# A second tiny write, from the first y tile into rows of the last output tile, in an interleaving copy kernel

## Chip, cores and metric

One core of one Trainium2 chip. The metric is the device time of one execution in microseconds (us). The core ran alone.

## The reference

```
x, y: (32, 256, 1024) float32
result[..., 0::2] = x
result[..., 1::2] = y          # (32, 256, 2048) float32
```

There is no arithmetic: 33.55 MB are read from x, 33.55 MB from y, and 67.11 MB are written. The values only have to change places, which VectorE does in SBUF.

## The kernel before

The flat arrays are cut into 8 tiles of 128 partitions x 8192 elements. Each tile is loaded with one DMA for x and one for y (4 MB each, on SP's queue, called q1 in the profile), interleaved in two halves by VectorE with two strided copies each, and stored with one DMA for each half (4 MB each, on ACT's queue, q10). Every pool has two buffers.

```
xpool, ypool, opool: bufs=2
zero = wpool.tile([16, 128]); nc.vector.memset(zero, 0.0)
first = out rows 0..15 of the first tile, 128 elements (512 B) each
nc.scalar.dma_start(out=first, in_=zero)          # the early tiny write

for lw in lwidths:                                 # 8 tiles
    xtile, ytile = ...
    nc.sync.dma_start(out=xtile, in_=xs)
    nc.sync.dma_start(out=ytile, in_=ys)
    for each half (soff = 0, 4096):
        otile = opool.tile([P, 2 * WS])
        nc.vector.tensor_copy(out=otile[:, 0::2], in_=xsub)
        nc.vector.tensor_copy(out=otile[:, 1::2], in_=ysub)
        nc.scalar.dma_start(out=os_, in_=otile)
# ... (the first x load is moved ahead of the opening barrier)
```

The framework adds the semaphores: a load waits until the buffer's last reader is done (the third y load goes out at 26.52 us, the copies that read its buffer end at 26.50), and a store to rows that an earlier DMA wrote waits until that one has landed.

Of the kernel before, what the change touches and what calls it, by code (L numbers as in the profile page):

```python
# [2 lines left out]

# [4 lines left out]


@with_exitstack
def _interleave(
    ctx: ExitStack,
    tc: tile.TileContext,
    x: bass.AP,
    y: bass.AP,
    out: bass.AP,
):
    nc = tc.nc
    P = 128  # L20

    total = 1
    for s in x.shape:
        total *= s

    WL = 8192
    WS = 4096

    xf = x.rearrange("b s d -> (b s d)")
    yf = y.rearrange("b s d -> (b s d)")  # L30
    of = out.rearrange("b s d -> (b s d)")

    fp32 = mybir.dt.float32

    xpool = ctx.enter_context(tc.tile_pool(name="xp", bufs=2))
    ypool = ctx.enter_context(tc.tile_pool(name="yp", bufs=2))
    opool = ctx.enter_context(tc.tile_pool(name="op", bufs=2))

    lwidths = [WL] * (total // P // WL)
    assert sum(lwidths) == total // P  # L40


    wpool = ctx.enter_context(tc.tile_pool(name="wp", bufs=1))
    zero = wpool.tile([16, 128], fp32, name="zero")
    nc.vector.memset(zero, 0.0)  # L45
    first = dataclasses.replace(of, offset=0, ap=[[2 * WL, 16], [1, 128]])
    nc.scalar.dma_start(out=first, in_=zero)

    start = 0
    for lw in lwidths:  # L50
        xtile = xpool.tile([P, WL], fp32, name="xtile")[:, :lw]
        ytile = ypool.tile([P, WL], fp32, name="ytile")[:, :lw]

        xs = dataclasses.replace(xf, offset=start, ap=[[lw, P], [1, lw]])
        ys = dataclasses.replace(yf, offset=start, ap=[[lw, P], [1, lw]])
        nc.sync.dma_start(out=xtile, in_=xs)
        nc.sync.dma_start(out=ytile, in_=ys)

        soff = 0
        while soff < lw:  # L60
            width = min(WS, lw - soff)
            otile = opool.tile([P, 2 * WS], fp32, name="otile")[:, : 2 * width]
            os_ = dataclasses.replace(
                of,
                offset=2 * start + 2 * soff,
                ap=[[2 * lw, P], [1, 2 * width]],
            )
            xsub = xtile[:, soff : soff + width]
            ysub = ytile[:, soff : soff + width]
# [3 lines that stand above are left out]
            soff += width  # L73

        start += P * lw
    assert start == total


def kernel(tc, x, y, out):
    nc = tc.nc  # L80
    _interleave(tc, x, y, out)
    tc.close()
    tc.compile()  # L83


    blocks = nc.main_func.blocks
    opening = blocks[0].instructions
    at, moved = next(
        (b, i)
        for b in blocks[1:]  # L90
        for i in b.instructions
        if i.engine == mybir.EngineType.SP and i.opcode == "DMACopy"
    )
    assert not moved.sync_info.on_wait
    body = at.instructions
    body.remove(moved)
    gate = next(
        n
        for n, i in enumerate(opening)
        if i.engine == mybir.EngineType.SP and i.opcode == "Drain"  # L100
    )
    opening.insert(gate, moved)
    at.instructions = body
    blocks[0].instructions = opening


# [1 line left out]
_INS = ['x', 'y']  # L108
_OUTS = [((32, 256, 2048), 'float32')]


# [23 lines left out]
```

## Time and profile before

| | before |
|---|---|
| time, median of the first 3 runs | 315.98 us (315.83 to 316.15) |
| span of the profiled execution | 313.8 us |
| busy VectorE | 23% |
| time of the packets on q1 + q10, share of 16 DMA engines | 49.9% + 49.5% |
| third y load issued | 26.52 us |
| first store issued | 24.32 us |

In profile lines DVE is VectorE, POOL GpSimd, SP SyncE and ACT ScalarE; a q behind the name (SPq) means the engine's instruction sequencer, which issues its DMAs, and L56 is line 56 of the kernel. A packet is one row of a DMA, here 32 KB for a full one (the trace before has 4096 of these, 128 for each of the 32 large DMAs), carried by one of the 16 DMA engines; a DMA lands when all its packets are done (the last packet of the first y load, one of 4 bytes, starts at 21.62 us, and the load lands at 21.97).

### The profile page before, as it was taken

What the parts mean: (1) busy time and instruction counts of PE and PEld (TensorE: products, weight loads), DVE (VectorE), ACT (ScalarE), POOL (GpSimd) and SP (SyncE); (2) the same over time, 40 slices, a digit from 0 to 9 for tenths busy, and PEclk for the clock granted to TensorE, in tenths of its full rate; (3) what the DMA queues carried; (4) which work ended last, traced back from release to release, by engine and by line L of the source; (5) the groups of instructions that cost most, each with busy time, mean ns of one, the idle gap of its engine ahead of it and who ended that gap; (6) DMA issues with size and microseconds to landing.
All of it is one profiled execution on the core that took longest, in us unless ns stands there. A gap on an engine that the chain in (4) does not pass through costs nothing.

```text
span 313.8 us, 152 instructions
## 1 busy us (share of the span) xinstructions
DVE 72.8 (23%) x33; POOL 0.2 (0%) x4
## 2 busy tenths in 40 slices
DVE  0433002231032410325003150130501305023500
POOL 0000000000000000000000000000000000000000
DMA  8999999999999999999999999999999999999997
GB/s 339 464 405 397 468 401 464 405 464 405 464 405 464 405 459 409 451 418 451 418 434 434 430 439 426 443 413 455 401 468 401 468 401 468 401 468 401 464 405 334
DMA packets 4640, 134.23 MB, mean 428 GB/s; under 512 B 528, under 2 KB 544, under 8 KB 544
## 3 DMA queue, kind: packets, MB, share of 16 engines
q1 hardware_dynamic: 2304, 67.11, 49.9%
q10 hardware_dynamic: 2336, 67.12, 49.5%
HBM read 67.11 MB, written 67.12 MB: 428 GB/s over the span
## 4 chain that ended last, share of the span: by engine, by line
DMA 83%; DVE 11%; DVEq 1%; issue 0%
DMA out_dram<-otile 76%; DMA ytile<-in_y_dram 7%; DVE otile L71 6%; DVE otile L70 5%; DVEq L83 1%; DVEq L70 0%
## 5 line engine op out<-in xcount | busy, mean ns | idle before, releaser
L70 DVE COPY otile<-xtile 128x4096 f32<-128x4096 f32 x16 | 36.6, 2295 | 184.9 <-DMA out_dram<-otile 173.7
L71 DVE COPY otile<-ytile 128x4096 f32<-128x4096 f32 x16 | 36.6, 2292 | 39.8 <-DMA ytile<-in_y_dram 39.8
L45 DVE MEMSET zero<- 16x128 f32 x1 | 0.2, 165 | 0.9 <-PEq L119 0.9
L119 POOL MEMSET const-bfloat16-1.0<- 128x1 bf16 x1 | 0.1, 102 | 0.0
L119 POOL MEMSET const-uint8-127<- 128x1 uint8 x1 | 0.1, 102 | 0.0
L119 POOL MEMSET const-float32-0.0<- 128x1 f32 x1 | 0.1, 99 | 0.2 <-issue 0.2
L119 POOL MEMSET const-float32-1.0<- 128x1 f32 x1 | 0.1, 99 | 0.0
## 6 DMA issues: line engine op xcount, KB each, us to landing
out_dram<-otile ACTq DMA_DIRECT2D x16, 4096.0 KB, 29.1
xtile<-in_x_dram SPq DMA_DIRECT2D x8, 4096.0 KB, 43.6
ytile<-in_y_dram SPq DMA_DIRECT2D x8, 4096.0 KB, 60.7
out_dram<-zero ACTq DMA_DIRECT2D x1, 8.0 KB, 6.3
```

Of the source, the lines that this page charges most:

```text
L45: nc.vector.memset(zero, 0.0)
L70: nc.vector.tensor_copy(out=otile[:, 0::2], in_=xsub)
L71: nc.vector.tensor_copy(out=otile[:, 1::2], in_=ysub)
L83: tc.compile()
L119: nc = _bacc.Bacc("TRN2", target_bir_lowering=False, num_devices=1)
```

## The change

A second write of 16 rows of 512 B is issued on ACT's queue as soon as the first y tile lands. Its rows lie in the last output tile, whose real store overwrites them some 260 us later. The early write stays. No comment in the code gives a reason. The likely intent is to touch a far part of the output early, so that the real store finds it ready.

```
         nc.sync.dma_start(out=ytile, in_=ys)
+
+        if start == 0:
+            late = dataclasses.replace(
+                of, offset=2 * (total - P * WL), ap=[[2 * WL, 16], [1, 128]]
+            )
+            nc.scalar.dma_start(out=late, in_=ytile[:16, :128])
```

## The prediction

> **What bounds the kernel now.** I read the page first (busy rows, queues, chain), then the issues of the DMAs, then the waits, then the first 30 us as a timeline, then stretches of the span, and last the single packet records behind them.
>
> The two DMA queues come first, because no compute engine is busy for more than a quarter of the time:
>
> ```profile
> span 313.8 us, 152 instructions
> ...
> DVE 72.8 (23%) x33; POOL 0.2 (0%) x4
> ...
> DMA  8999999999999999999999999999999999999997
> ...
> q1 hardware_dynamic: 2304, 67.11, 49.9%
> q10 hardware_dynamic: 2336, 67.12, 49.5%
> ```
>
> The loads (q1) and the stores (q10) together take 49.9 + 49.5 = 99.4% of the time of all 16 DMA engines. The row of digits says the same: only the first and the last slice of 7.8 us are below nine tenths. What is left to win without moving fewer bytes or moving them faster is 0.6% of 313.8 us, about 1.9 us. The packet records confirm it: every full-size packet is one 32 KB row, it takes 1.213 us at its fastest and almost always, and each engine has 4096 / 16 = 256 of them, so 256 x 1.213 = 310.5 us. The first packet starts 1.0 us into the span and the last one ends 1.1 us before its end; the remaining 1.2 us are 16 slow first packets and one hitch of which more below.
>
> The rate does not depend on the mix of loads and stores, which the stretches show (columns: stretch, length, busy VectorE, busy GpSimd, clock, DMA share, GB/s):
>
> ```profile
> 30.00:70.00 40.00, 7.10 (x4) 0.00 (x0) 1.00 1.00 433
> ...
> 148.00:224.00 76.00, 16.72 (x8) 0.00 (x0) 1.00 1.00 431
> 224.00:266.00 42.00, 11.97 (x6) 0.00 (x0) 1.00 1.00 431
> 266.00:298.00 32.00, 8.79 (x4) 0.00 (x0) 1.00 1.02 440
> ```
>
> In steady state loads and stores alternate; in the last of these stretches the loads run out (the last y tile lands at 287.67) and the rate stays. So shifting a load against a store by a few microseconds changes the order of the work and not its sum, as long as neither queue's lack of work empties an engine. The timeline agrees: the x load of a tile is issued at 69.81, 108.53, 147.26, 185.97 and 224.71, a period of 38.7 us for the 16.78 MB of a tile, 433 GB/s.
>
> The waits look different at first sight:
>
> ```profile
> DVE otile L70 <- DMA out_dram<-otile: 173.7, 14, 21.6
> DVE otile L71 <- DMA ytile<-in_y_dram: 39.8, 8, 5.2
> ```
>
> VectorE waits for stores and loads for most of the span. It is not the bottleneck, so these waits cost nothing by themselves: they are the DMA engines' backlog seen from the other side.
>
> [...]16 x 32768 B / 1.213 us = 432 GB/s while busy. [...]the tiny early write, issued on ACT's queue while loads run on SP's, has its 512 B packets at 5.3 to 5.9 us and its completion packets one load packet (1.2 us) later. [...]the tiny write took 6.3 us from issue to landing, because it stood behind 32 KB packets. The measured 6.3 is what I use. [...]the 16 packets of the early write took 27 ns each.
>
> **The change, part by part.** Nothing is removed. Added is one DMA on ACT's queue, from partitions 0 to 15 of the first y tile, 16 rows of 512 B (8 KB), into the first columns of 16 rows of the last output tile. The real store of that tile overwrites it much later.
>
> ```profile
> out_dram<-zero ACTq DMA_DIRECT2D x1, 8.0 KB, 6.3
> ...
> 1.06 0.42 ACTq L47 DMA_DIRECT2D out_dram<-zero  x1
> ...
> 16.80 0.33 SPq L56 DMA_DIRECT2D xtile<-in_x_dram  x1
> 22.00 4.50 DVE L71 COPY otile<-ytile 128x4096 f32<-128x4096 f32 x2 [5.22 <-DMA ytile<-in_y_dram]
> 24.32 2.56 ACTq L72 DMA_DIRECT2D out_dram<-otile  x2
> 26.52 0.33 SPq L57 DMA_DIRECT2D ytile<-in_y_dram  x1
> ```
>
> 1. Issue. The y tile lands at 21.97, when VectorE's copy (22.00) is released too. ACT's sequencer has nothing to do until the first store at 24.32, which waits for that copy. The new issue takes some 0.34 to 0.42 us (the other issues of ACT), so it is out at about 22.4, 1.9 us before the first store wants the sequencer. On the path: 0.
>
> 2. Work of the DMA engines. 16 rows over 16 engines is one packet each, 27 ns, and one completion packet, 9 ns (both as the early write's packets measure). That is 36 ns on each engine, and the engines are the bound, so it counts fully: +0.04 us.
>
> 3. A reader more on the first y buffer. The third y load, into the same buffer, is issued at 26.52 as soon as VectorE has read the tile. It must now also wait until the new write has read it, which is known only when that has landed. With the early write's 6.3 us that is 22.0 + 6.3 = 28.3, so this load is issued some 1.8 us later, at about 28.4. At that time SP's queue still holds the second x and y tiles and the third x tile, issued at 1.16, 1.63 and 16.80: 12.6 MB less what has gone (from 20 to 28 us about 3.4 MB), over 20 us of work for all engines. The late load lands behind them as before, about 94 us. SP's next issue is at 69.81. On the path: 0.
>
> 4. A second writer of the last tile's rows. The store of the first half of the last tile, at about 290 us, must wait for the new write, which has landed some 260 us before. 0.
>
> 5. Completion semaphores. DMAs take turns over eight semaphores, and each waits until the one eight places before has landed. The kernel issues four DMAs for each tile, so eight places back is the same kind of DMA two tiles back, with or without one DMA inserted near the start: only the first round changes partners, and these have landed long before. 0.
>
> Sum: 315.98 + 0.04 = 316.02 us, which I round to 316.0.
>
> **The rivals.**
> (a) The new wait on the y buffer becomes a real stall: the third y load is late and an engine runs dry. For it: it is a new wait of about 1.8 us and loads are issued in order. Against it: the backlog of over 20 us in step 3. If it bit, the time would be 317 to 318, still inside 2%.
> (b) The write takes away the hitch at the start of the stores, or causes another. In the packet records, the 16 load packets that start at 27.3 to 27.7 us take 1.69 to 1.88 us in place of 1.21; right after them, at 29.1, the first store packets begin. That is the only such place after the start, worth about 0.6 us on each engine. If an earlier write on the queue took that start upon itself, the time would be 315.4; if it made a second one, 316.6. Against both: the early tiny write was on the same queue at 5.3 us, and its neighbours took 1.21 us, so a tiny write neither causes the hitch nor spares it.
> (c) The intent of the change, I suppose, is that a page or row of the output touched early makes the first real store there cheaper. Against it: if first touches cost anything, the store packets of the tiles that nobody touched before would show it, and from 29.1 us to the end no full-size packet, load or store, took over 1.4 us. There is nothing to warm. Gain 0.
> (d) The first store waits for the new write, too, because the dependence between the two is taken too coarsely: it would go out at about 28.4 in place of 24.3. Against it: stores to other rows do not wait for each other now. Even so, loads would fill the engines meanwhile, the stores would be 4 us behind in order, and the end would move by little: 316.0 to 317.
>
> **Range and chances.** The three runs before spread from 315.83 to 316.15, so a median is good to 0.15 us or so. Around 316.0 I leave 0.6 us for the hitch of (b) on either side and lean slightly upwards for (a) and (d): 315.5 to 316.6. Faster by 2% would need 6.3 us, over three times what the idle share of the engines holds; I give it 0.003. Slower by 2% needs 6.3 us of idle engines, or a slower rate for all packets, from one DMA of 8 KB; I give it 0.007. Within 2%: 0.99.
>
> **What would show it.** In the profile of the changed kernel: a DMA of 8 KB on ACT's queue issued at 22.0 to 22.1 and landing 5 to 7 us later; the first store still issued at 24.3; the third y load at 28 to 29 us with a wait on the new write; q10 with 2368 packets (32 more: 16 of data, 16 of completion) and the shares of q1 and q10 still 99.4% together; x loads from the fourth on still 38.7 us apart; the last store issued at about 298.3 and the end at about 313.8. I would be wrong if the digits of the DMA row fell below 9 somewhere in the middle, if the period of a tile changed, or if packets of 32 KB took other than 1.21 us.

Cut from the prediction is what it cited on the DMA engines from elsewhere; of that paragraph the measured figures stand. No term of the sum is cut: the five steps give 0 + 0.04 + 0 + 0 + 0, so that 315.98 becomes 316.02. Three things that it says in passing are in the records of the trace before. The tiny write "stood behind 32 KB packets": each of its 16 packets of 512 B starts within 4 ns of the end of a 32 KB packet, at 5.27 to 5.86 us, while its issue was over at 1.48. The "completion packets" are records of 4 bytes and 9 ns, 16 for each of the 33 DMAs, 528 in all. And the eight semaphores of step 5 are those numbered 100 to 107, which the 33 DMAs take in turn in the order of the program: the stores issued at 57.64, 135.09 and 212.54 us, two tiles apart, all have number 100, and before the first of them ACT waits for number 100, which the first x load has.

## The result

| | before | changed |
|---|---|---|
| median | 316.12 us (315.83 to 316.93, 6 runs) | 316.04 us (315.64 to 317.36, 6 runs) |
| ratio | | 1.0001, 95% interval 0.9979 to 1.0023 |

Ratios are the mean time of one kernel's runs over that of the other's of the same rounds, so they are not quite the ratio of the medians quoted.

The execution that was profiled first was by chance the slowest of the six (317.36 us, span 315.6). The changed kernel was therefore run again, unedited, with five rounds (the run called "again" below). That trace has a span of 313.9 and is the one to hold against the trace before. First its page, the lines that answer to those of the prediction:

```profile
span 313.9 us, 152 instructions
...
DMA  8999999999999999999999999999999999999997
...
DMA packets 4673, 134.24 MB, mean 428 GB/s; under 512 B 545, under 2 KB 577, under 8 KB 577
...
q1 hardware_dynamic: 2304, 67.11, 49.9%
q10 hardware_dynamic: 2368, 67.13, 49.5%
```

q10 has the 32 packets more that were foretold (2336 became 2368; the one packet besides in the total is an instruction fetch), and the two shares and all forty digits of the DMA row are what they were. Then the issue of the new write (KB, us from issue to landing), followed by the timeline of the same trace (start, length, what):

```profile
out_dram<-ytile ACTq DMA_DIRECT2D x1, 8.0 KB, 6.1
```

```profile
16.84 0.33 SPq L56 DMA_DIRECT2D xtile<-in_x_dram  x1
22.01 0.32 ACTq L65 DMA_DIRECT2D out_dram<-ytile  x1
22.01 4.50 DVE L79 COPY otile<-ytile 128x4096 f32<-128x4096 f32 x2 [5.20 <-DMA ytile<-in_y_dram]
24.34 2.56 ACTq L80 DMA_DIRECT2D out_dram<-otile  x2
28.14 0.33 SPq L57 DMA_DIRECT2D ytile<-in_y_dram  x1
```

The write goes out at 22.01 in the gap that ACT had, the first store at 24.34 (24.32 before), and the third y load at 28.14 instead of 26.52: the one event of these that the change moved. What SP waited for before its y loads (us in total, times, longest) names the reason, the new write:

```profile
SPq L57 <- DMA out_dram<-ytile: 10.9, 1, 10.9
SPq L57 <- DVE otile L79: 9.0, 5, 1.8
```

That y tile still lands at 94.04 (94.05 before), and nothing after it moved by more than 0.04 us. The later x loads start at 108.52, 147.24, 185.97 and 224.69, against 108.53, 147.26, 185.97 and 224.71 before, and the last store is issued at 298.3 in both.

The slower trace shows where the excess of that run comes from. Sorting its packet records by engine (each engine's packets follow each other without a gap), 15 of the 16 engines end their last 32 KB packet between 312.2 and 312.6 us, as in the trace before (312.3 to 312.7). One ends at 314.4: it had load packets of 1.25 to 2.19 us at 27.9, 33.8, 48.6, 67.1, 126.7 and 226.0 us, where 1.21 is normal (at 27.9 the other engines' packets were slow too, 1.6 to 1.9 us). The run ends with its slowest engine. The trace of "again" has no such packets after the first store, so they do not come with the change in every execution; what causes them is not known.

### The profile page after: what moved, and what is told of

It reads as the page before. It is cut to its first block, busy times and chain, and to the rows that moved or that the text cites. A ratio compares the mean times of both kernels' runs of the same rounds, so it can differ in the third digit from the quotient of the medians.

```text
span 315.6 us, 152 instructions
## 1 busy us (share of the span) xinstructions
DVE 72.8 (23%) x33; POOL 0.2 (0%) x4
## 3 DMA queue, kind: packets, MB, share of 16 engines
q10 hardware_dynamic: 2368, 67.13, 49.3%
## 4 chain that ended last, share of the span: by engine, by line
DMA 83%; DVE 11%; DVEq 1%; issue 0%
DMA out_dram<-otile 76%; DMA ytile<-in_y_dram 7%; DVE otile L79 6%; DVE otile L78 5%; DVEq L91 1%; DVEq L78 0%
```

## The experiments

Twelve runs were made, all correct; two of them (again, first_tile_again) repeat a kernel. In every diff, a minus line is the changed kernel.

### Is it really nothing, and does either tiny write do anything?

**again**: the changed kernel, no edit.

> The changed kernel once more, unedited, for a narrower interval and a second trace. My theory (16 DMA engines saturated, the write costs 36 ns on each): ratio 1.000, median 315.8 to 316.3. In the profile of the changed kernel one engine of the 16 ended 1.8 us after the others because five of its packets took 1.3 to 2.2 us; if that is chance, this trace has such packets elsewhere or not at all and the last 32 KB packet ends near 312.7 us; if the new write causes it, the same late engine comes back with the span near 315.6.

Measured: 315.78 us (315.68 to 316.22), ratio 0.9995, interval 0.9982 to 1.0008. The late engine did not come back: the 16 engines end between 312.2 and 312.7 us.

**none**: both tiny writes taken out.

```
-    nc.scalar.dma_start(out=first, in_=zero)
-            nc.scalar.dma_start(out=late, in_=ytile[:16, :128])
```

> Neither tiny write. My theory: 315.9 to 316.0, ratio 1.000, and the hitch of about 0.6 us at the first store packets stays. Rival (touching output rows early warms something): slower than the kernel before by 0.5 us or more, with full-size packets over 1.4 us at the start of tiles.

Measured: 316.19 us (315.77 to 316.33), ratio 1.0002, interval 0.9989 to 1.0016. There are no slow packets at the start of any tile, and the slow load packets just before the first store (1.5 to 2.1 us, at 27.4 to 27.9 us) are there as in the others, with a smaller group one packet earlier (14 packets of 1.25 to 1.96 us at 25.8 to 26.2 us; the trace before has five, of 1.31 to 1.58).

**late_only**: the new write without the early one.

```
-    nc.scalar.dma_start(out=first, in_=zero)
```

> The new write without the early one. My theory: 316.0, ratio 1.000. Rival (b), a small write on the queue before the first store moves or spares the hitch: the hitch at 27 us is gone and the time about 315.4, or there are two and 316.6.

Measured: 316.35 us (315.65 to 316.56), ratio 1.0006, interval 0.9992 to 1.002. The slow packets before the first store are there, at 27.3 to 27.8 us with the smaller group just before them, and no second set comes. With the two tiny writes present or absent in all four ways, no kernel differs from the one before beyond the intervals. Neither write warms anything that can be measured here.

### Does work put on the DMA engines count in full?

**wide**: the new write takes whole rows, 512 KB, one full packet for each engine. **wide_spread**: the same, read from every eighth partition instead of partitions 0 to 15.

```
-                of, offset=2 * (total - P * WL), ap=[[2 * WL, 16], [1, 128]]
-            nc.scalar.dma_start(out=late, in_=ytile[:16, :128])
+                of, offset=2 * (total - P * WL), ap=[[2 * WL, 16], [1, 8192]]
+            nc.scalar.dma_start(out=late, in_=ytile[:16, :8192])       # wide
+            nc.scalar.dma_start(out=late, in_=ytile[0:128:8, :8192])   # wide_spread
```

> The new write 64 times as wide: 16 rows of 32 KB, one full-size packet for each engine. My theory, that work on the saturated engines counts fully: +1.21 us, 317.2, ratio 1.0038. A rival in which an inserted write hides beside other work: 316.0. If the hitch belongs to the first full-size write packet of the run, it appears once, a little before this packet, and not again at the first store.

Measured: 319.83 us (319.32 to 319.87), ratio 1.0116, interval 1.0099 to 1.0133: +3.7 us, three times the 1.21 expected. The 16 packets of the write took 3.26 to 4.47 us, 3.87 in the mean, in place of 1.21. The rows were read from partitions 0 to 15; that choice of source was the next thing to vary, in wide_spread.

> The 512 KB write again, but its 16 rows are read from partitions 0, 8, 16 ... 120 in place of 0 to 15. In the run before, its 16 packets took 3.3 to 4.5 us each in place of 1.21 and the run grew by 3.7 us. [...] Theory two, that the first full-size store packet of a run is slow wherever it reads from: packets of 3.3 to 4.5 us and 319.8 again. Theory three, work alone: packets of 1.21 to 1.9 us, time 317.2.

(The first of its three theories is cut: it rested on a mechanism that no run of this case shows.)

Measured: 317.24 us (317.09 to 317.55), ratio 1.0034, interval 1.002 to 1.0048: by the ratio +1.1 us, which is about the bare work. All 16 packets took 1.21 to 1.22 us. The two writes stand in the lists of issues like this, first wide, then wide_spread:

```profile
out_dram<-ytile ACTq DMA_DIRECT2D x1, 512.0 KB, 10.7
```

```profile
out_dram<-ytile ACTq DMA_DIRECT2D x1, 512.0 KB, 8.2
```

Same bytes, same rows of the output, same place in the queue, and 2.5 us between the landings; the edit differs only in the source partitions. So theory three, work alone, held for the spread write. Theory two fell, since the spread write was the first full-size store of its run and not slow. The slow packets of wide (3.87 us in the mean) go with a source in partitions 0 to 15; why was not shown.

For the prediction the result is plain: a write on these engines is not hidden. Its size is what makes the change free: 512 KB cost 1.1 us (0.6 to 1.5 by the interval), and 8 KB is 1/64 of these bytes.

wide_spread also answers the question about the slow load packets at 27 us. They come before the wide write (25.0 to 25.7 us, 1.5 to 2.0 us each, and a smaller group at 23.4 to 24.1) and not again before the first store. In wide no load packet between 3 us and the write took 1.24 us or more: there the write's own packets were the slow ones, and only three load packets followed at 1.6 to 1.8 us. So the slow load packets come before the first full-size writes in all traces but this one.

### Is there slack for the held-back y load?

**gate_st1** and **gate_st3**: the third y load is held back much longer, by a tiny copy that goes ahead of it into the same buffer and waits for the second, or the fourth, store to land.

```
+        if start == 2 * P * WL:
+            landed = 16 rows x 128 elements of that store, in the output
+            nc.gpsimd.dma_start(out=ytile[:16, :128], in_=landed)
         nc.sync.dma_start(out=ytile, in_=ys)
```

> The changed kernel, with the third y load held back until the second store (second half of the first tile) has landed: a tiny copy of rows of that store into the y buffer goes ahead of the load. The load is issued at about 70 us in place of 28. My theory (over 20 us of queued loads, then two stores, cover it): 316.0 to 316.6, ratio 1.000 to 1.002, the DMA row stays at 9. Rival (a), that a late y load costs what it is late: far more than 320.

Measured: 316.75 us (316.57 to 317.77), ratio 1.0024, interval 1.0007 to 1.0041. From its timeline, the copy and then the load:

```profile
68.07 1.85 POOL L63 DMA_DIRECT2D ytile<-out_dram  x1 [67.63 <-DMA out_dram<-otile]
...
76.08 0.33 SPq L64 DMA_DIRECT2D ytile<-in_y_dram  x1
```

The load is issued at 76.08, which is 48 us later than in the changed kernel and later than I had expected (70). The x and y loads behind it went out at 76.5 and 77.1 (69.8 and 72.0 in the changed kernel). By the ratio all this costs 0.8 us, a little over the expected range, and no slice of the DMA row but the last falls below 9. So the 1.6 us by which the change delays the load is far inside the slack.

> The same gate on the fourth store: the third y load is issued at about 90 us, behind the fourth x and y loads, and lands when both queues have run out. My theory: an idle stretch of the DMA engines between the landing of this y tile (about 118 us) and the first packet of the next store, 4 to 5 us, and the run as much longer: 320 to 321.5, with a digit below 9 in one slice of the DMA row near 118 us. If the DMA row has no such slice and the time is still up, my account of the slack is wrong.

Measured: 321.08 us (320.65 to 321.79), ratio 1.0157, interval 1.0141 to 1.0173. Here the load comes too late. Stretches of this run (start:end, length, busy VectorE, busy GpSimd, clock, DMA share, GB/s) and the issue of the x load queued right behind the held-back y load:

```profile
100.00:107.00 7.00, 0.88 (x1) 0.28 (x1) 1.00 1.04 449
107.00:110.00 3.00, 1.42 (x1) 1.51 (x1) 1.00 0.42 178
110.00:114.00 4.00, 0.00 (x0) 0.00 (x0) 1.00 0.87 303
114.00:126.00 12.00, 3.73 (x2) 0.00 (x0) 1.00 1.00 429
```

```profile
110.30 0.38 SPq L56 DMA_DIRECT2D xtile<-in_x_dram  x1
```

The engines stand idle for 1.4 to 2.5 us each near 109 us, the packets that start again after it take 1.3 to 2.2 us, and the ones before the next store (at 126 to 130 us) are slow once more. The size was right, the place was not: I had put the hole at 118 us, after the landing of the y tile, and it opened before the load's issue at 109.88, because the fourth store landed only at 106.3 and the two loads queued meanwhile had run out. Still, this is what the harm of a late load looks like, and it is not in the changed kernel.

### What if the first store is late?

**first_tile**: the new write goes to rows of the first tile, so the first store must wait for it.

```
-                of, offset=2 * (total - P * WL), ap=[[2 * WL, 16], [1, 128]]
+                of, offset=0, ap=[[2 * WL, 16], [1, 128]]
```

> The new write goes to rows of the first output tile, so that the first store must wait until it has landed (rival (d) of the prediction made real). My theory, that the loads already queued fill the engines: first store issued at about 28.4 in place of 24.6, time 315.8 to 316.3, ratio 1.000. Rival, that a later first store lengthens the run: 317 to 320.

Measured: 318.84 us (runs of 320.11, 319.55, 315.66 and 318.13), ratio 1.0069, interval 1.002 to 1.0117. My theory missed here, and so did the rival as stated, since one run was at 315.66 (the slowest, which is the profiled one, is 1.4% above the fastest). The first store was issued at 28.20, as expected, and no slice of the DMA row but the last fell below 9, yet the steady rate was lower. The same stretches in the kernel before and in this one:

```profile
150.00:190.00 40.00, 9.09 (x4) 0.00 (x0) 1.00 1.00 433
190.00:230.00 40.00, 9.09 (x4) 0.00 (x0) 1.00 1.01 435
```

```profile
150.00:190.00 40.00, 8.99 (x4) 0.00 (x0) 1.00 1.00 423
190.00:230.00 40.00, 9.02 (x5) 0.00 (x0) 1.00 1.00 428
```

The engines are as busy as before (share 1.00) and move less: in the packet records, 441 store packets and 66 load packets took 1.24 us or more after 40 us, where the trace before has none. Four runs followed to find what it hangs on.

**first_tile_again**: the same kernel.

> The same kernel as first_tile, for the spread of its runs (318.84 median, 315.66 to 320.11) and a second trace. In the first trace the extra 3 us were store packets of 1.25 to 1.5 us in place of 1.21, on 11 of 16 engines. Theory one, the delayed first store always sets a slow pairing: all runs above 317. Theory two, chance in each execution: again a wide spread, some runs near 315.7, others near 320, and a trace of a run near 316 without such packets. Theory three, the first job met a disturbed chip: all runs at 316.

Measured: 316.68 us (315.94 to 318.56, 6 runs), ratio 1.0033, interval 1.0006 to 1.0059. Theory two held, chance in each execution: a wide spread again, and the profiled run, at 315.94, has 34 slow packets in place of 507.

**chain_y2** and **chain_x3**: the first store is made later still, by two tiny writes of the y tile, or three of the x tile, to the same rows of the first tile (offset=0 as in first_tile), each waiting for the one before.

```
-            nc.scalar.dma_start(out=late, in_=ytile[:16, :128])
+            nc.scalar.dma_start(out=late, in_=ytile[:16, :128])   # chain_y2: twice
+            nc.scalar.dma_start(out=late, in_=xtile[:16, :128])   # chain_x3: three times
```

> Two writes to the first tile one after the other, each waiting for the one before: the first store is issued at about 34 us, some 10 us late, after about 30 load packets on each engine in place of 22 (24 in first_tile). If lateness of the first store itself costs: more than first_tile, 320 to 325. If it is the pairing of the loads' rows with the stores' rows (24 is three whole DMAs): 316.0 to 316.6, spread under 1 us. If it is chance once the stores are late: spread of several us as in first_tile.

> Three chained writes to the first tile from the first x tile, which lands at 12.3 us: the first store is issued at about 30.5 us, after about 27 load packets on each engine. Lateness alone: about 320. Pairing of rows: 316.0 to 316.6. Chance: spread of several us.

Measured: chain_y2 315.97 us (315.87 to 316.14), ratio 1.0, interval 0.9987 to 1.0013, first store issued at 34.86. chain_x3 316.05 us (315.7 to 316.38), ratio 1.0002, interval 0.999 to 1.0014, first store issued at 31.89. A later first store costs nothing in itself. (The x tile's writes in chain_x3 also hold back the third x load, to 31.89 from 16.8, so it is not the first store alone that moves there.) Counting in the packet records how many load packets each engine had done before its first store packet gives this table (one profiled execution of each kernel; the records do not number the engines, and the sorting is unsure where several engines end a packet together):

| kernel | load packets before the first store packet | spread of runs, us |
|---|---|---|
| before, changed (both jobs), none, late_only | 22 | 315.49 to 317.36, 70 runs |
| first_tile, first_tile_again | 25 to 26 (some engines 39 in the first trace, by this sorting) | 315.66 to 320.11, 10 runs |
| chain_x3 | 28 | 315.7 to 316.38, 5 runs |
| chain_y2 | 30 to 32 | 315.87 to 316.14, 5 runs |

**extra_dve**: reaches the count of 25 without a new wait on a write and with the new write still in the last tile, by repeating two copies on VectorE.

```
             nc.vector.tensor_copy(out=otile[:, 1::2], in_=ysub)
+            if start == 0:
+                nc.vector.tensor_copy(out=otile[:, 1:6144:2], in_=ysub[:, :3072])
```

> The changed kernel with two repeated copies on VectorE (12288 of the 65536 elements of the first y tile's interleave done twice), so that the first store is issued at about 28.1 us with no new wait on a write and the new write still in the last tile. In first_tile and its repeat every engine (but one) had its first store packet after 25 or 26 load packets and the runs spread from 315.7 to 320.1; at 22, 28 and 30 to 32 they did not spread. If that count is what matters: 25 or 26 here, runs from 315.7 up to 318 or 320, store packets of 1.25 to 1.5 us in a slow run's trace. If first_tile's wait or its write to the first tile matters instead: 316.0 with a spread under 1 us although the count is 25.

Measured: 317.85 us (316.53 to 320.48, 6 runs), ratio 1.0043, interval 1.002 to 1.0067. The count is 25 or 26 (but for one engine, by this sorting), the spread is there, and the profiled run (320.48) has 253 slow store packets and 126 slow load packets. From its timeline and its stretches:

```profile
28.33 30.20 ACTq L84 DMA_DIRECT2D out_dram<-otile  x3
```

```profile
150.00:190.00 40.00, 8.99 (x4) 0.00 (x0) 1.00 1.00 424
190.00:230.00 40.00, 8.99 (x4) 0.00 (x0) 1.00 1.01 428
```

So it needs neither the wait nor those rows: a start of the stores 25 to 26 packets behind the loads goes with a slower and less steady packet rate in some executions. Of the 16 runs of these kernels 8 lie above 317.36 us, which is the highest of the 70 runs at 22; the highest of the 10 at 28 to 32 is 316.38. One thing sets this offset apart in the records. Each large DMA has eight packets on each engine (128 over 16), and 25 is three whole loads and one packet. In first_tile_again no engine moves two loads or two stores in a row between 60 and 270 us, so a load's eight packets keep step with a store's eight; in the kernel before, in again and in chain_x3 one step in eight is of the same kind, so the two are shifted. That this step is the cause is argued, not shown: the profiled run in which it shows clearly was the shortest of its six (315.94). Why some executions suffer was not settled; a packet's record does not say what it waits for. In the changed kernel the count stays at 22.

## Why the prediction was right

- **The bound.** Both queues together at 99.4% of 16 engines, before and after. wide_spread shows that work added to them is paid: 1.1 us for one full packet on each, 1.21 foretold.
- **Step 1, the issue.** Out at 22.01 in 0.32 us; the first store at 24.34 against 24.32. Right.
- **Step 2, the work.** The new packets took 27 ns each. The mean over the 16 engines of the end of the last full packet was 312.41 us in the trace before and in the trace of "again", so the foretold 0.04 us is below what two traces can tell apart. It is not confirmed as a size. That the median of 316.04 lies within 0.02 of the sum of 316.02 is luck: the kernel before came out at 316.12 in this job, 0.14 above the 315.98 that the sum starts from.
- **Step 3, the y buffer.** Foretold about 28.4, measured 28.14 (28.36 in the slower trace). gate_st1 held the load to 76 us for 0.8 us, gate_st3 showed where the slack ends.
- **Steps 4 and 5, the second writer and the semaphores.** The last store was issued at 298.3 in both; no new wait shows. The 34 DMAs of the changed kernel take the same eight semaphores in turn.
- **Rival (a)** fell with gate_st1 (48 us of delay cost 0.8 us), **(b)** with none and late_only (the slow packets before the first store stay, whatever tiny writes there are), **(c)** with none.
- **Rival (d)** did not happen, as foretold, but its price was told too low: "316.0 to 317" for a first store at 28.4, and the run that made it so had a median of 318.84, its repeat 316.68. The sentence behind it, that shifting loads against stores "changes the order of the work and not its sum", holds at the offsets of 22, 28 and 30 to 32 packets and fails at 25 to 26. The same goes for its "the rate does not depend on the mix". The change left the count at 22, so this did not touch the result.
- **The range** of 315.5 to 316.6 holds the medians of both jobs (316.04 and 315.78). Single runs went up to 317.36, by one late engine.
- **Small slips in its reading**, without effect on the sum: the slow load packets at 27 us are not "the only such place" (five at 25.9 to 26.1 us took 1.31 to 1.58), and the fastest full-size packet took 1.211 us, not 1.213.

## What to carry to other kernels

Where the DMA engines are busy at 99% of the span, price an added transfer by its packets on one engine (in wide_spread 1.21 us foretold, 1.1 measured; check in the trace that they ran at the usual rate, for in wide they took three times as long, 3.87 us), and ask of each new wait only how much work is still queued ahead of it. A delay of one load may be nearly free by tens of microseconds (0.8 us for 48 here), but a delay that changes the offset between two interleaved streams can change the rate itself (423 GB/s in place of 433 over 40 us of first_tile), so look at the packets' durations and at the spread of the runs, and not only at idle time. Where rows of 32 KB were read from SBUF for a DMA, spreading them over the partitions saved 2.6 us (wide against wide_spread); rows of 512 B were not tried spread, and from partitions 0 to 15 their packets took 27 ns.

## What else the traces show

- The start of the stores is slow: the load packets just before the first full-size store packets took about 0.6 us longer on each engine, and this moved with the first store (from 27.3 us before, 31.0 in first_tile_again, 34.5 in chain_x3), and came a second time in gate_st3 (126 to 130 us) after the stores had paused. Only in wide were the load packets spared.
- An 8 KB write on ACT's queue, behind 32 KB packets on the same engines, took 6.0 to 7.1 us from issue to landing in the traces. The 8 KB copy that GpSimd issues took 8.0 us in gate_st1, where the DMA share was 0.98 (66 to 76 us), and 3.1 us in gate_st3, where it was 0.42 (107 to 110 us).
